# Where the weight halves start in SBUF: a fixed offset modulo 512 bytes for each of two matmul forms

## The chip, the cores and the metric

One Trainium2 chip, one of its cores. The metric is the device time in microseconds (us) of one execution of the whole kernel. The kernel before was timed three times: median 2776.59 us, from 2774.45 to 2779.73.

## The reference, cut to what matters

Two transformer blocks over 256 tokens of width 2048, all in float32. The first has an adaptive-norm modulation, a recurrent branch, a sliding-window attention branch and a gated feed-forward; the second has a gated linear attention and another gated feed-forward. Nearly all the arithmetic is products of the activations with large weight matrices:

```python
h = modulate(rms_norm(x, norm1_g[l]), sh1, sc1)
proj = h @ w_in[l] + b_in[l]                       # 2048 x 11264
...
merged = gate_lru * (y_lru @ w_lru_out[l]) + gate_attn * (y_attn @ w_attn_out[l])
x = x + g1 * (merged @ w_o[l])
h2 = modulate(rms_norm(x, norm2_g[l]), sh2, sc2)
gate, up = jnp.split(h2 @ w_ffn_in[l], 2, axis=-1)  # 2048 x 2 * 5632
x = x + g2 * ((jax.nn.silu(gate) * up) @ w_ffn_out[l])
...                                                 # second block: proj = h @ w_in (GLA), w_out,
...                                                 # and a second feed-forward of the same sizes
```

The modulation vectors are `silu(c) @ ada_w + ada_b`, a single row times a 2048 x 12288 matrix.

## The kernel before, in words

**The product.** Every big weight matrix is cut into chunks of 512 x 512, which lie in SBUF as `[128, 4, 512]` float32 (tile `raw`, 1 MB). A chunk is loaded by SyncE's queue (`load`, L152) and split into two float32r parts: ScalarE copies a half of the chunk into `hi` (L165), VectorE writes the remainder into `lo` (L167). Each `hi` or `lo` tile is half a chunk, `[128, 2, 512]`, 4096 bytes in each partition. The pools hold three of each of `raw`, `hi` and `lo`. The activations are split in the same way once, in tiles of class `Pair`. A product is then three matmuls: hi by hi, hi by lo, lo by hi, accumulated in PSUM by `accumulate`.

**Two forms.** `accumulate` has two forms.
- *Narrow* (256 moving columns, L189, L191, L193): a 128 x 128 block of the weights is the stationary operand and the 256 tokens of the activations stream through. The stationary operands in order are hi, hi, lo; the streams are the activations' hi, lo, hi. A chunk is 48 matmuls.
- *Wide* (512 moving columns, `tokens=True`, L182 to L184): 128 tokens of the activations are stationary and 512 columns of the weights stream through. The streams in order are the weights' hi, lo, hi. A chunk is 24 matmuls. It is used for the two feed-forward input matrices (PSUM names `fgps`, `fups`), for the values of both attentions (`gvps`, and `e` at L182 to L184).

Every matmul record (PE in the profile) has a weight-load record (PEld) ahead of it, which loads the stationary operand while the matmul before is running.

**Order.** A chunk's load, split and matmuls are issued in program order, chunk after chunk; the pools' buffers let loads and splits run ahead of the matmuls. `high_priority(offset=lead[0])` puts loads and splits ahead in the schedule. Small work (attention, recurrence, norms) is interleaved by the generator tasks that `pump` advances. The modulation's matrix is not multiplied on TensorE: `matvec` loads 512 KB pieces of it into tiles `mvw` (L234; on the POOL queue in the first stage, on SP's after that) and VectorE accumulates them into `mva` (L237, L239), 16 pieces for a strip, then a few one-column matmuls sum the partitions (`mvp`, L251). The pool `mvw` has `MVS = 6` buffers.

**Where tiles begin.** The pools are laid out one behind the other in each partition: `const`, `xpool`, `act` (24 slots of 4096 bytes, which hold the activations' `Pair` tiles), `small`, `mvw` (4096 bytes each), `rawp` (8192 each), `hip`, `lop` (4096 each). All of these sizes but that of `small` are multiples of 512. `small` takes 4096 (`ssq`, two) + 1024 (`std`) + 2048 (`inv`, two) + 256 (`st`, two) + 64 (`invp`, two of 32) + 3 x 1024 (`war`, `warh`, `warl`) + 1024 (`ms4`) + 1024 (`alr`) = 12608 bytes, 320 beyond a multiple of 512. So, modulo 512, all `hi` and `lo` tiles begin 320 bytes behind the activations' tiles, which is the same as 192 bytes ahead of them. The blocks within the tiles are whole multiples of 512 bytes apart, so this holds for every operand of the two forms.

Of the kernel before, what the change touches and what calls it, by code (L numbers as in the profile page):

```python
# [12 lines left out]
F32R = mybir.dt.float32r  # L13
# [5 lines left out]
P = 128  # L19
# [3 lines left out]
NG = NK // 4  # L23
EPS = 1e-6
PREP = 2000
SLOTS, MVS, RAWS, HIS, LOS = 24, 6, 3, 3, 3
NEG = -3.0e38
HEADS = 16
KVH = 4
# [20 lines left out]
def block_pair_kernel(ctx: ExitStack, tc: tile.TileContext, a: dict):  # L50
# [8 lines left out]
    hip = ctx.enter_context(tc.tile_pool(name="hip", bufs=HIS))  # L59
    lop = ctx.enter_context(tc.tile_pool(name="lop", bufs=LOS))  # L60
# [8 lines left out]
    def f32(ap):  # L69
        return ap.bitcast(F32)  # L70
# [79 lines left out]
    def load(ap):  # L150
        raw = rawp.tile([P, 4, 512], F32, tag="raw", name="raw")
        nc.sync.dma_start(raw, ap)  # L152
        return raw

    lead = [0]

    def split(ap):

        parts = []
        with tc.high_priority(offset=lead[0]):  # L160
            raw = load(ap)
            for b in range(2):
                rb = raw[:, 2 * b:2 * b + 2, :]
                hi = hip.tile([P, 2, 512], F32R, tag="hi", name="hi")
                nc.scalar.activation(hi, rb, AF.Copy)  # L165
                lo = lop.tile([P, 2, 512], F32R, tag="lo", name="lo")
                nc.vector.tensor_tensor(lo, rb, f32(hi), ALU.subtract)  # L167
                parts.append((hi, lo))
        return parts

    def accumulate(ps, ap, src, first, last, tokens=False):

        parts = split(ap)
        for kk in range(4):
            hi, lo = parts[kk // 2]
            wk = kk % 2
            fst, lst = first and kk == 0, last and kk == 3
            if tokens:
                for t in range(2):
                    tsl = slice(t * P, (t + 1) * P)  # L180
                    xh, xl = src.hi(kk)[:, tsl], src.lo(kk)[:, tsl]
                    nc.tensor.matmul(ps[t], xh, hi[:, wk, :], start=fst, stop=False)  # L182
                    nc.tensor.matmul(ps[t], xh, lo[:, wk, :], start=False, stop=False)  # L183
                    nc.tensor.matmul(ps[t], xl, hi[:, wk, :], start=False, stop=lst)  # L184
                continue
            for f in range(4):
                wsl = slice(f * P, (f + 1) * P)
                o = ps[f // 2][:, f % 2, :]
                nc.tensor.matmul(o, hi[:, wk, wsl], src.hi(kk), start=fst and f % 2 == 0,  # L189
                                 stop=False, skip_group_check=True)  # L190
                nc.tensor.matmul(o, hi[:, wk, wsl], src.lo(kk), start=False, stop=False,  # L191
                                 skip_group_check=True)
                nc.tensor.matmul(o, lo[:, wk, wsl], src.hi(kk), start=False, stop=lst,  # L193
                                 skip_group_check=True)
# [4 lines left out]
    def project(chunks, src, name, tokens=False):  # L199


        ps = banks(name, tokens)
        n = len(chunks)
        for c in range(n):
            accumulate(ps, chunks[c], src[c], c == 0, c == n - 1, tokens)
            if c < n - 1:
                pump()
        return ps
# [247 lines left out]
    for q in range(NG):  # L456
# [3 lines left out]
        for g, ks in plan[q]:  # L460
# [7 lines left out]
            for k in ks:  # L468
                if g in held:
                    accumulate(ps, a["w_in"][g, k], h[k], k == 0, k == NG - 1, tok)  # L470
                else:
                    accumulate(ps, a["w_in"][g, k], h[k], k == ks[0], k == ks[-1])
                for st in ahead[:share]:
                    st()
                if ahead and len(ahead) <= share:
                    next_h()
                ahead = ahead[share:]
                lead[0] = PREP
                if q == NG - 1 and k < ks[-1]:
                    pump()  # L480
# [585 lines left out]
```

## Time and profile before

| What | Value |
|---|---|
| median of three runs | 2776.59 us |
| the profiled execution's own time | 2775.35 us |
| its span, first to last instruction | 2773.6 us |
| granted TensorE clock, mean | 0.999 |
| PE (matmuls) | 2710.8 us, 98% of the span, 18612 records |
| PEld (weight loads) | 2489.2 us, 90% |
| DVE | 1784.8 us, 64% |
| ACT | 1321.3 us, 48% |
| HBM read over the span | 597.06 MB |

How to read it: the span is what the profiler saw between the first and the last instruction, 1.75 us less than that execution's own time. Matmul records overlap, since each is shown from its start to its modelled end behind the array; how fast the matmuls really follow each other is seen from the starts of consecutive records, called the *step* below, and not from their durations.

### The profile page before, as it was taken

How to read it: one execution, taken by the hardware profiler on the slowest of the kernel's cores; microseconds unless marked ns; L12 is line 12 of the kernel's file. 1: busy time of each engine (PE TensorE's matmuls, PEld its weight loads, DVE VectorE, ACT ScalarE, POOL GpSimd, SP SyncE). 2: the span in 40 equal slices, each digit the busy share in tenths (PEclk: the TensorE clock that was granted, in tenths of full speed). 3: DMA queues.
4: the chain of work that ended last, by engine and by line, in shares of the span. 5: the costliest groups of instructions: out<-in, count | busy, mean ns of one | idle time of the engine just before them, and what ended most of it. 6: DMA issues, size and time to landing. Idle time of an engine off the chain costs nothing.

```text
span 2773.6 us, 43912 instructions
## 1 busy us (share of the span) xinstructions
PE 2710.8 (98%) x18612; PEld 2489.2 (90%) x18612; DVE 1784.8 (64%) x2000; ACT 1321.3 (48%) x1531; POOL 25.7 (1%) x52
## 2 busy tenths in 40 slices
PE   4999999999999999999999999999999999999999
PEld 4999899999999788899888999899988889988899
DVE  8887966977876865444444677866654444444544
ACT  3446537873445444434444555555554443344443
POOL 1100000000000000000000000000000000000000
PEclk9999999999999999999999999999999999999999
DMA  9974784768875776555555544445555555555554
GB/s 364 368 301 149 261 324 175 282 241 324 326 283 181 271 259 217 180 190 193 183 192 186 190 169 168 147 144 182 192 188 182 183 190 189 198 182 189 185 196 160
DMA packets 100165, 602.00 MB, mean 217 GB/s; under 512 B 11120, under 2 KB 11632, under 8 KB 40576
## 3 DMA queue, kind: packets, MB, share of 16 engines
q1 hardware_dynamic: 93056, 574.03, 58.2%
q0 software_dynamic: 6912, 25.17, 2.3%
q8 instruction: 145, 2.38, 0.3%
q14 instruction: 52, 0.43, 0.0%
HBM read 597.06 MB, written 2.10 MB: 216 GB/s over the span
## 4 chain that ended last, share of the span: by engine, by line
PE 91%; DVE 5%; ACT 1%; issue 1%; DMA 1%; SPq 0%; DVEq 0%; ACTq 0%
PE fops L189 6%; PE fops L191 6%; PE fops L193 6%; PE fgps L184 6%; PE fgps L183 6%; PE fgps L182 6%; PE fups L184 5%; PE fups L183 5%; PE fups L182 5%; DVE lo L167 2%; PE part L189 2%; PE part L191 2%; PE part L193 2%; DVE mva L239 1%; DMA mvw<-ada_w 1%
## 5 line engine op out<-in xcount | busy, mean ns | idle before, releaser
L167 DVE TENSOR_TENSOR lo<-raw,hi 128x1024 fp32r<-128x1024 f32 x928 | 1134.4, 1223 | 899.3 <-ACT hi L165 897.5
L165 ACT ACTIVATE hi<-raw 128x1024 fp32r<-128x1024 f32 x928 | 982.8, 1060 | 1285.8 <-PE fups L184 280.6
L189 PE MATMUL fops<-hid,hi 128*128 128x256 f32 x1408 | 389.0, 276 | 0.0
L193 PE MATMUL fops<-hid,lo 128*128 128x256 f32 x1408 | 388.8, 276 | 0.0
L191 PE MATMUL fops<-hid,hi 128*128 128x256 f32 x1408 | 388.8, 276 | 0.0
L183 PE MATMUL fups<-lo,h 128*128 128x512 f32 x704 | 275.9, 392 | 0.9 <-DVE lo L167 0.9
L184 PE MATMUL fups<-hi,h 128*128 128x512 f32 x704 | 276.7, 393 | 0.0
L182 PE MATMUL fups<-hi,h 128*128 128x512 f32 x704 | 274.2, 390 | 0.0
L184 PE MATMUL fgps<-hi,h 128*128 128x512 f32 x672 | 264.9, 394 | 0.0
L182 PE MATMUL fgps<-hi,h 128*128 128x512 f32 x672 | 264.6, 394 | 0.0
L191 PEld LDWEIGHTS fops<-hid,hi 128*128 128x128 f32 x1408 | 264.3, 188 | 0.0
L189 PEld LDWEIGHTS fops<-hid,hi 128*128 128x128 f32 x1408 | 264.3, 188 | 0.0
L193 PEld LDWEIGHTS fops<-hid,lo 128*128 128x128 f32 x1408 | 264.3, 188 | 0.0
L183 PE MATMUL fgps<-lo,h 128*128 128x512 f32 x672 | 263.3, 392 | 0.0
L239 DVE SCALAR_TENSOR_TENSOR mva<-mvw,cact,mva 128x1024 f32<-128x1024 f32 x180 | 230.2, 1279 | 18.7 <-DMA mvw<-ada_w 17.0
L183 PEld LDWEIGHTS fups<-lo,h 128*128 128x128 f32 x704 | 132.2, 188 | 31.3 <-DVE lo L167 1.3
L182 PEld LDWEIGHTS fups<-hi,h 128*128 128x128 f32 x704 | 132.2, 188 | 29.3
L184 PEld LDWEIGHTS fups<-hi,h 128*128 128x128 f32 x704 | 132.3, 188 | 27.4
L183 PEld LDWEIGHTS fgps<-lo,h 128*128 128x128 f32 x672 | 126.3, 188 | 27.4
L182 PEld LDWEIGHTS fgps<-hi,h 128*128 128x128 f32 x672 | 126.3, 188 | 26.3
L184 PEld LDWEIGHTS fgps<-hi,h 128*128 128x128 f32 x672 | 126.3, 188 | 26.0
L189 PE MATMUL part<-h,hi 128*128 128x256 f32 x512 | 145.6, 284 | 0.1
(322 smaller groups left out, 5440.6 us busy)
## 6 DMA issues: line engine op xcount, KB each, us to landing
raw<-w_in SPq DMA_DIRECT2D x88, 1024.0 KB, 4.9
raw<-w_ffn_in SPq DMA_DIRECT2D x88, 1024.0 KB, 4.8
raw<-ffn_w_gu SPq DMA_DIRECT2D x88, 1024.0 KB, 4.8
mvw<-ada_w SPq DMA_DIRECT2D x144, 512.0 KB, 6.5
raw<-gla_w_in SPq DMA_DIRECT2D x48, 1024.0 KB, 4.8
raw<-w_ffn_out SPq DMA_DIRECT2D x44, 1024.0 KB, 4.9
raw<-ffn_w_down SPq DMA_DIRECT2D x44, 1024.0 KB, 4.9
mvw<-ada_w POOLq DMA_DIRECT2D x48, 512.0 KB, 8.4
```

What stands on the lines that cost most here:

```text
L165: nc.scalar.activation(hi, rb, AF.Copy)
L167: nc.vector.tensor_tensor(lo, rb, f32(hi), ALU.subtract)
L182: nc.tensor.matmul(ps[t], xh, hi[:, wk, :], start=fst, stop=False)
L183: nc.tensor.matmul(ps[t], xh, lo[:, wk, :], start=False, stop=False)
L184: nc.tensor.matmul(ps[t], xl, hi[:, wk, :], start=False, stop=lst)
L189: nc.tensor.matmul(o, hi[:, wk, wsl], src.hi(kk), start=fst and f % 2 == 0, stop=False, skip_group_check=True)
L191: nc.tensor.matmul(o, hi[:, wk, wsl], src.lo(kk), start=False, stop=False, skip_group_check=True)
L193: nc.tensor.matmul(o, lo[:, wk, wsl], src.hi(kk), start=False, stop=lst, skip_group_check=True)
L239: nc.vector.scalar_tensor_tensor(state["acc"], w, col(k), state["acc"], ALU.mult, ALU.add)
```

## The change

The `hi` and `lo` tiles become 1152 elements long (4608 bytes, nine times 512) and only 1024 of them are used, from an offset that depends on the form. In the narrow form `hi` starts at 0 and `lo` at 32 elements (128 bytes). In the wide form both start at 48 elements (192 bytes). So, modulo 512, the narrow `hi` stays 192 bytes ahead of the activations, the narrow `lo` is 64 bytes ahead of them, and the wide `hi` and `lo` begin level with them. The six longer tiles take 3 KB more in each partition; `MVS` goes from 6 to 5, which frees 4 KB. The count, the operands' shapes and the order of matmuls, loads and splits in the program are the same.

```diff
-SLOTS, MVS, RAWS, HIS, LOS = 24, 6, 3, 3, 3
+SLOTS, MVS, RAWS, HIS, LOS = 24, 5, 3, 3, 3
...
-    def split(ap):
+    def halfbuf(pool, name, tokens):
+        t = pool.tile([P, 1024 + P], F32R, tag=name, name=name)
+        at = 48 if tokens else {"hi": 0, "lo": 32}[name]
+        return t[:, at:at + 1024].rearrange("p (b n) -> p b n", b=2)
+
+    def split(ap, tokens=False):
...
-                hi = hip.tile([P, 2, 512], F32R, tag="hi", name="hi")
+                hi = halfbuf(hip, "hi", tokens)
                 nc.scalar.activation(hi, rb, AF.Copy)
-                lo = lop.tile([P, 2, 512], F32R, tag="lo", name="lo")
+                lo = halfbuf(lop, "lo", tokens)
                 nc.vector.tensor_tensor(lo, rb, f32(hi), ALU.subtract)
...
-        parts = split(ap)
+        parts = split(ap, tokens)
```

## The prediction

> **What bounds the kernel.** I read the page's busy times and clock first, then the groups of instructions, then the timeline of PE alone (for the step from one matmul's start to the next), then the waits.
>
> ```profile
> span 2773.6 us, 43912 instructions
> PE 2710.8 (98%) x18612; PEld 2489.2 (90%) x18612; DVE 1784.8 (64%) x2000; ACT 1321.3 (48%) x1531; POOL 25.7 (1%) x52
> PEclk9999999999999999999999999999999999999999
> L167 DVE TENSOR_TENSOR lo<-raw,hi 128x1024 fp32r<-128x1024 f32 x928 | 1134.4, 1223 | 899.3 <-ACT hi L165 897.5
> L165 ACT ACTIVATE hi<-raw 128x1024 fp32r<-128x1024 f32 x928 | 982.8, 1060 | 1285.8 <-PE fups L184 280.6
> ```
>
> PE is busy in 98% of the span at full clock, and the two splitting engines each stand idle for some 900 us or more: VectorE behind ScalarE, ScalarE behind the matmuls that free its buffers. So the step of the matmuls sets the time. Nothing that the change does to the split's own speed reaches the end before DVE, at 64%, runs out of room.
>
> How many matmuls there are of each form comes from the groups, with shapes kept apart:
>
> ```profile
> L189 PE MATMUL fops<-hid,hi 128*128 128x256 f32 x1408 | 389.0, 276 | 0.0
> L189 PE MATMUL lops<-yr,hi 128*128 128x256 f32 x256 | 72.0, 281 | 0.0
> L189 PE MATMUL glps<-h,hi 128*128 128x256 f32 x256 | 72.0, 281 | 0.0
> L191 PE MATMUL wops<-m,hi 128*128 128x256 f32 x256 | 71.9, 281 | 0.0
> L191 PE MATMUL ups<-h,hi 128*128 128x256 f32 x256 | 71.2, 278 | 0.0
> L191 PE MATMUL part<-h,hi 128*128 128x256 f32 x512 | 143.0, 279 | 0.0
> L183 PE MATMUL fups<-lo,h 128*128 128x512 f32 x704 | 275.9, 392 | 0.9 <-DVE lo L167 0.9
> L183 PE MATMUL fgps<-lo,h 128*128 128x512 f32 x672 | 263.3, 392 | 0.0
> L183 PE MATMUL gvps<-lo,h 128*128 128x512 f32 x128 | 50.1, 392 | 0.0
> L183 PE MATMUL e<-lo,h 128*128 128x512 f32 x32 | 12.6, 394 | 0.0
> L183 PE MATMUL fgps<-lo,gx 128*128 128x512 f32 x32 | 12.6, 392 | 0.0
> ```
>
> L183 is one of three wide lines: (704 + 672 + 128 + 32 + 32) x 3 = 4,704 wide matmuls, 196 chunks. The 928 splits are 464 chunks, so 268 are narrow: x 48 = 12,864. The last column to look at is the mean duration: 276 ns for `fops`, 281 for the same shape in `lops`, `glps`, `wops`, and 278 or 279 for `ups` and `part`. The timeline shows that this goes with the step. Its first and last lines, over four stretches without a break:
>
> ```profile
> 1159.82 0.28 PE L191 MATMUL fops<-hid,hi 128*128 128x256 f32 x1
> ...
> 1165.94 0.28 PE L191 MATMUL fops<-hid,hi 128*128 128x256 f32 x1
> ...
> 799.79 0.28 PE L189 MATMUL wops<-m,hi 128*128 128x256 f32 x1
> ...
> 805.92 0.28 PE L191 MATMUL wops<-m,hi 128*128 128x256 f32 x1
> ...
> 1299.71 0.39 PE L184 MATMUL fgps<-hi,h 128*128 128x512 f32 x1
> ...
> 1308.87 0.39 PE L182 MATMUL fups<-hi,h 128*128 128x512 f32 x1
> ...
> 200.79 0.40 PE L183 MATMUL e<-lo,h 128*128 128x512 f32 x1
> ...
> 204.99 0.40 PE L183 MATMUL e<-lo,h 128*128 128x512 f32 x1
> ```
>
> There are 54, 52, 40 and 18 steps between these lines: 6.12/54 = 113.3 ns, 6.13/52 = 117.9 ns, 9.16/40 = 229.0 ns, 4.20/18 = 233.3 ns. So each form has two steps, a better and a worse one, 4 to 5 ns apart, though in both the operands stand at the same offset modulo 512. Which one runs is not a matter of that offset alone; a stretch falls into one and stays there. The worse narrow one holds all of `lops`, `glps` and `wops` (nine groups of 256, 2,304 matmuls) and, by means of 278 and 279 between 276 and 281, about half of `ups`, `gps` and `part` (another 1,100 to 1,600); I take 3,400.
>
> The form sum: 12,864 x 113.3 = 1457 us, 3,400 x 4.6 = 16, 4,704 x 229.0 = 1077, together 2550 of the 2773.6; the opening and the small work are the rest and the change doesn't touch their operands.
>
> **The change part by part.** What could be had at all is bounded by two other kinds of matmul in the same trace: `lrps`, narrow streams with a load of only 16 columns, and `ss3p`/`ss4p`, full float32, whose 256 columns come at half the rate and so stream as long as 512 wide ones.
>
> ```profile
> 1647.06 0.28 PE L787 MATMUL lrps<-h,warl 128*16 128x256 f32 x1
> ...
> 1648.98 0.28 PE L786 MATMUL lrps<-h,warh 128*16 128x256 f32 x1
> ...
> 1630.49 0.59 PE L294 MATMUL ss3p<-ss,onesd 128*128 128x256 f32 x2
> ...
> 1631.78 0.59 PE L295 MATMUL ss4p<-ss,onesd 128*128 128x256 f32 x2
> ```
>
> `lrps`: 17 steps in 1.92 us, 112.9 ns, within the reading's error the better narrow step. Its stationary blocks are 64 bytes each, one behind the other, so they begin at every multiple of 64 modulo 512 in turn, and the step does not follow. `ss3p`: six records in 1.29 us, 215 ns.
>
> *Narrow, hi left and lo moved by 128 bytes (L193's load).* The better step of 113.3 is what `lrps` has with an eighth of the weight read, so I see nothing to win there: 0. What can go is the worse step: 3,400 x 4.6 ns = 15.6 us, if the new place of `lo` keeps the stream out of it. On the other side, all narrow matmuls could fall into it: (12,864 - 3,400) x 4.6 = +43.5 us. I take -15.6, the end that a third of the way would still bring beyond the timing's noise, because the worse step is a matter of how load and stream stand to each other, and the change sets exactly that.
>
> *Wide, both parts level with the stationary activations (L182 to L184).* The nearest rows are the two steps of this form itself, and twice the better narrow step: 226.6. At that rate the wide matmuls save 229.0 - 226.6 = 2.4 ns, x 4,704 = 11 us. The far end is `ss3p`'s 215: 14 ns, 66 us. On the other side stands the worse wide step: +4.3 ns, 20 us. I take -11, as the row nearest in rate of reading is the narrow stream, not the half-rate one.
>
> *MVS 6 to 5.* Piece k of a strip is now loaded when piece k-5 has been used, one VectorE step of about 1.28 us later. On SP the wait also holds up the `raw` loads queued behind it.
>
> ```profile
> PE mvp L251 <- DVE mva L239: 36.7, 3, 34.4
> DVE mva L239 <- DMA mvw<-ada_w: 17.0, 13, 4.1
> POOL mvw L234 <- DVE mva L239: 95.9, 45, 27.2
> SPq L234 <- DVE mva L239: 47.2, 28, 4.7
> SPq L152 <- DVE lo L167: 2328.9, 453, 17.2
> PE gkps L193 <- DVE lo L167: 2.3, 3, 0.9
> ```
>
> Of PE's 36.7 us behind the modulation 34.4 are the opening, where one strip must be summed before any product; the other two waits are 2.3 us together. The opening can move by up to one VectorE step, 1.3 us. In twelve strips at most 12 x 1.28 = 15 us could show, if PE waited at each; it waits at almost none. A `raw` load stands 2328.9/453 = 5.1 us for its buffer on average, so an SP wait that grows from 4.7 us at most by 1.3 is mostly covered; with that cover gone it would be PE's wait on `lo`, 2.3 us in the largest row now. One load fewer in flight could also leave `raw` a little more of the DMA: -1. I take +1, ends -1 and +15.
>
> *Longer tiles, other addresses in the split.* ScalarE and VectorE write the same 1024 elements, 928 times each; taken at 0, hidden by the idle 899 and 1286 us above. Even 5% more on VectorE's 1134 us would be 57 us of its own idle time.
>
> Sum: -15.6 - 11 + 1 = -25.6. The profiled execution took 2775.35 us (1.75 beyond its span), so it would take 2749.8; the median of the runs is 1.24 above that execution, which makes 2751.
>
> Against the trace stands a rule of the Trainium skill, "TensorE: Matmul & The Clock Gate", Back-to-back issue gap: N/2.4 + 2.5 ns for a single warm matmul, 109.2 and 215.8 ns here. The trace shows 113.3 and 229.0 instead, and 215 only in the half-rate form. By that rule, were both forms to reach it, the estimate would be -53 - 16 - 62 + 1 = -130 us, about 2646; `lrps` speaks against its narrow part.
>
> **The rivals.**
> - *Nothing happens.* The start modulo 512 doesn't matter to PE at all, and the time is that of before with one `mvw` buffer less: 2776.6 + 1 = 2778. For it: `lrps` goes through all eight starts at one step, and the two steps of each form occur at one and the same offset. Against it: those loads are short, and something that depends on how load and stream stand to each other makes the worse step. The Trainium skill has a rule that gives this outcome, "SBUF — State Buffer", Who interferes with whom: PE's stream and its weight load have a read port each, and PE waits on nobody. The two steps at equal shape, count and clock are hard to square with it.
> - *Slower: the wide form locks into its worse step.* With stream and load level, both begin on the same part of a 512-byte period within a few ns of each other. If that is the bad stand, each wide matmul costs 233.3 as in `e` at 200 us: 4,704 x 4.3 = +20 us, +1 for MVS: 2798. Against it: the better step is by far the commoner in this form. It decides alone from 5.5/4,704 = 1.2 ns a matmul on. If the narrow form falls into its worse step as well, 2841.
> - *Much faster: the wide stream loses its whole surplus* and steps at 215 like the half-rate one: -66 - 15.6 + 1, 2696. Against it: full-rate streams never step better than at 112.9 for half the columns, twice which is 226.
>
> **How the numbers follow.** Chances: the forecast with gains of some 6 to 40 us 0.37; much faster 0.12; nothing 0.25; slower by the wide form 0.17; slower in both 0.09. A change below 0.2%, 5.5 us, can't be told from none (the three runs lie 5.3 us apart). From "nothing", 0.02 may end on either side by chance of which stretches fall into the worse step, and 0.01 of the slower ones ends within: faster 0.50, same 0.24, slower 0.26. Predicted: 2751, with 2735 to 2771 as its own range. The range of all reaches from 2715 (which leaves out the most of "much faster") to 2798 (which leaves out "slower in both").
>
> **What would show it.** Right: `lops`, `glps` and `wops` at a mean of 276 ns; narrow steps of 113.3 throughout; wide steps of about 226 to 227; PE's waits as they are. Wrong: wide durations up towards 397 and steps of 233 (the slower rival); both forms' steps unmoved (nothing happens); a wide step below 220 or a narrow one below 112 (more to gain than I allow). A new PE wait on `mvp` in the opening or on `lo` while strips are loaded would mean that I priced the lost buffer too low.

## The result, and the profile after

The changed kernel takes 2761.12 us in the median (2757.35 to 2761.36), against 2777.45 us for the kernel before measured beside it (2774.45 to 2779.73): a ratio of 0.9939, with a 95% interval from 0.9921 to 0.9956. It is faster by 16 us, 0.6%; the prediction said 2751, 10 us less. The profiled execution took 2761.13 us, with a span of 2759.4 us, 14.2 less than before.

The page's busy times and its largest VectorE group. All lines of the product stand 8 lower in the changed file: narrow L197, L199, L201; wide L190 to L192; the split L173 and L175; the modulation's sum L247.

```profile
span 2759.4 us, 43921 instructions
PE 2691.7 (98%) x18612; PEld 2478.1 (90%) x18612; DVE 1783.9 (65%) x2000; ACT 1321.7 (48%) x1531; POOL 25.7 (1%) x52
L175 DVE TENSOR_TENSOR lo<-raw,hi 128x1024 fp32r<-128x1024 f32 x928 | 1134.4, 1223 | 871.2 <-ACT hi L173 869.2
```

PE is still busy in 98% of a shorter span. The split costs VectorE the same 1223 ns a tile, so the new addresses cost it nothing. Its idle time ahead of this group fell from 899 to 871 us, and its waits for pieces of the modulation matrix grew by 13 us (below).

The groups by shape of the kernel after (busy time and mean ns of one, after the bar):

```profile
L197 PE MATMUL fops<-hid,hi 128*128 128x256 f32 x1408 | 389.0, 276 | 0.0
L197 PE MATMUL lops<-yr,hi 128*128 128x256 f32 x256 | 70.8, 276 | 0.0
L197 PE MATMUL glps<-h,hi 128*128 128x256 f32 x256 | 70.9, 277 | 0.0
L199 PE MATMUL wops<-m,hi 128*128 128x256 f32 x256 | 70.7, 276 | 0.0
L199 PE MATMUL ups<-h,hi 128*128 128x256 f32 x256 | 70.7, 276 | 0.0
L191 PE MATMUL fups<-lo,h 128*128 128x512 f32 x704 | 273.9, 389 | 0.0
L191 PE MATMUL fgps<-lo,h 128*128 128x512 f32 x672 | 262.2, 390 | 0.0
```

`lops`, `glps` and `wops` came down from 281 ns to 276 or 277, where `fops` already was. The wide groups went from 392 to 389 or 390. The timeline of PE gives the step behind that: first and last line of three stretches of the kernel after without a break, in `glps`, `wops` and the wide form, with 55, 55 and 40 steps between them.

```profile
699.74 0.28 PE L197 MATMUL glps<-h,hi 128*128 128x256 f32 x1
...
705.97 0.28 PE L199 MATMUL glps<-h,hi 128*128 128x256 f32 x1
...
799.74 0.28 PE L199 MATMUL wops<-m,hi 128*128 128x256 f32 x1
...
805.97 0.28 PE L201 MATMUL wops<-m,lo 128*128 128x256 f32 x1
...
1299.77 0.39 PE L192 MATMUL fups<-hi,h 128*128 128x512 f32 x1
...
1308.84 0.39 PE L190 MATMUL fups<-hi,h 128*128 128x512 f32 x1
```

6.23/55 = 113.3 ns twice, where `wops` had 117.9 before; 9.07/40 = 226.8 ns, where it was 229.0.

Taken over all records of the two traces, from each matmul's start to the next one's (a narrow step between 116 and 130 ns counted as the worse one):

| | before | after | difference |
|---|---|---|---|
| narrow: steps in all | 1484.1 us | 1473.4 us | -10.7 us |
| narrow: how many in the worse step | 3,390 of 12,807 | 319 of 12,809 | |
| narrow: pauses of over 130 ns, in all | 30.0 us | 32.2 us | +2.2 us |
| narrow: mean of the better step | 113.34 ns | 113.34 ns | |
| wide: steps in all | 1068.9 us | 1059.0 us | -9.9 us |
| wide: mean step | 229.0 ns | 226.9 ns | |
| everything else on PE | 182.1 us | 187.9 us | +5.9 us |
| first matmul | | | 0.6 us later |

The rows of both forms' steps in all, of everything else and of the first matmul add up to -14.1, the change of the span. The first holds two things: the worse steps, 3,390 at 4.5 ns above the better one before and 319 at 5.6 after, which is 15.1 less 1.8, so -13.3; and the longer pauses. About 23 us were gained and 9 given back. Some of what gives them back is seen in PE's and VectorE's waits, totals in us, times and the longest:

```profile
PE mvp L259 <- DVE mva L247: 38.0, 3, 35.0
PE aops L201 <- DVE lo L175: 2.5, 2, 1.9
DVE mva L247 <- DMA mvw<-ada_w: 30.4, 26, 3.1
```

The opening wait on `mvp` has grown from 36.7 us to 38.0, VectorE stands 30.4 us instead of 17.0 for pieces of the modulation matrix, and a wait of `aops` on `lo` has grown from 0.4 to 2.5 us. The longest of its two comes about so (start and duration in us; in brackets, what the engine stood idle for before):

```profile
354.92 1.06 ACT L173 ACTIVATE hi<-raw 128x1024 fp32r<-128x1024 f32 x1 [1.65 <-PE aops L199]
360.11 1.28 DVE L247 SCALAR_TENSOR_TENSOR mva<-mvw,cact,mva 128x1024 f32<-128x1024 f32 x1 [3.13 <-DMA mvw<-ada_w]
361.31 1.22 DVE L175 TENSOR_TENSOR lo<-raw,hi 128x1024 fp32r<-128x1024 f32 x1
362.59 0.39 PE L201 MATMUL aops<-ya,lo 128*128 128x256 f32 x1 [1.92 <-DVE lo L175]
```

The chunk was there in time: counted in order, this copy `hi` is the one that this `lo` needs, and it was done at 355.98 us. But VectorE stood 3.13 us for a piece of the modulation matrix, whose sum comes ahead of the split in its order, and PE stood 1.92 us behind that.

The other large part is the granted clock. The trace of the kernel before has one stretch of 3.4 us at half the clock (from 132 us), the trace of the kernel after has four (from 82, 134, 321 and 960 us). Three more of them are 3 x 3.4 x 0.5 = 5 us, an estimate. Two of them are shown with the next experiment.

### The profile page after: what moved, and what is told of

Read it like the earlier page. It is cut to its first block, busy times and chain, and to the rows that moved or that the text cites. A ratio compares the mean times of both kernels' runs of the same rounds, so it can differ in the third digit from the quotient of the medians.

```text
span 2759.4 us, 43921 instructions
## 1 busy us (share of the span) xinstructions
PE 2691.7 (98%) x18612; PEld 2478.1 (90%) x18612; DVE 1783.9 (65%) x2000; ACT 1321.7 (48%) x1531; POOL 25.7 (1%) x52
## 4 chain that ended last, share of the span: by engine, by line
PE 88%; DVE 5%; DMA 3%; issue 3%; ACT 1%; POOL 0%; SPq 0%; DVEq 0%; POOLq 0%; ACTq 0%
PE fgps L191 6%; PE fgps L190 6%; PE fgps L192 6%; PE fops L197 6%; PE fops L201 6%; PE fops L199 6%; PE fups L192 5%; PE fups L190 5%; PE fups L191 5%; DMA mvw<-ada_w 3%; DVE lo L175 2%; PE part L199 1%; PE part L197 1%; PE part L201 1%; ACT hi L173 1%
## 5 line engine op out<-in xcount | busy, mean ns | idle before, releaser
L175 DVE TENSOR_TENSOR lo<-raw,hi 128x1024 fp32r<-128x1024 f32 x928 | 1134.4, 1223 | 871.2 <-ACT hi L173 869.2
L173 ACT ACTIVATE hi<-raw 128x1024 fp32r<-128x1024 f32 x928 | 983.1, 1060 | 1263.2 <-PE fups L192 274.5
L197 PE MATMUL fops<-hid,hi 128*128 128x256 f32 x1408 | 389.0, 276 | 0.0
L201 PE MATMUL fops<-hid,lo 128*128 128x256 f32 x1408 | 388.9, 276 | 0.0
L199 PE MATMUL fops<-hid,hi 128*128 128x256 f32 x1408 | 388.8, 276 | 0.0
L190 PE MATMUL fups<-hi,h 128*128 128x512 f32 x704 | 274.0, 389 | 0.0
L192 PE MATMUL fups<-hi,h 128*128 128x512 f32 x704 | 273.9, 389 | 0.0
L190 PE MATMUL fgps<-hi,h 128*128 128x512 f32 x672 | 264.7, 394 | 0.0
L199 PEld LDWEIGHTS fops<-hid,hi 128*128 128x128 f32 x1408 | 264.3, 188 | 0.0
L201 PEld LDWEIGHTS fops<-hid,lo 128*128 128x128 f32 x1408 | 264.3, 188 | 0.0
L197 PEld LDWEIGHTS fops<-hid,hi 128*128 128x128 f32 x1408 | 264.3, 188 | 0.0
L192 PE MATMUL fgps<-hi,h 128*128 128x512 f32 x672 | 263.1, 391 | 0.0
L247 DVE SCALAR_TENSOR_TENSOR mva<-mvw,cact,mva 128x1024 f32<-128x1024 f32 x180 | 230.5, 1280 | 32.3 <-DMA mvw<-ada_w 30.4
L190 PEld LDWEIGHTS fups<-hi,h 128*128 128x128 f32 x704 | 132.1, 188 | 27.5
L192 PEld LDWEIGHTS fups<-hi,h 128*128 128x128 f32 x704 | 132.1, 188 | 27.5
L192 PEld LDWEIGHTS fgps<-hi,h 128*128 128x128 f32 x672 | 126.3, 188 | 26.0
L190 PEld LDWEIGHTS fgps<-hi,h 128*128 128x128 f32 x672 | 126.5, 188 | 25.0
L197 PE MATMUL part<-h,hi 128*128 128x256 f32 x512 | 145.4, 284 | 0.0
```

The lines of the kernel that those rows point to most:

```text
L247: nc.vector.scalar_tensor_tensor(state["acc"], w, col(k), state["acc"], ALU.mult, ALU.add)
```

## The experiments

Two theories stood at the start. One: the two places act separately, each on its own form, and the lost `mvw` buffer takes a part of the gain back. The rivals: the gain is the longer tiles or a reshuffle of the schedule, so that any change of the kind shifts stretches between the two steps; or one of the places brings it all. (The longer tiles by themselves are answered below: `narrow_only` and `wide_only` both have them, and each leaves the step of the other form as it was.) "Before" is measured beside each kernel on the same chip; for the first four its median was 2779.75 us.

### The change with its buffer back

```diff
-SLOTS, MVS, RAWS, HIS, LOS = 24, 5, 3, 3, 3
+SLOTS, MVS, RAWS, HIS, LOS = 24, 6, 3, 3, 3
```

> The new offsets in both forms, with the sixth mvw buffer back. Theory (offsets give the whole gain, the lost buffer takes some of it back, by the trace about 4 to 5 us of waits): ratio to the kernel before 0.9925, some 2757 us; narrow steps of 113.3 and wide of 226.9 as with the change; PE's waits of some 2 us on lo in aops and the longer opening gone. Rival (the buffer costs only the 1 us that was predicted, the extra waits are chance): 0.994, the same as the change. Rival (the gain came from the schedule with five buffers): no gain left, 1.000.

Measured: 2755.35 us, ratio 0.9911 [0.9898, 0.9924]; span 2753.5 us; 316 narrow matmuls in the worse step, wide step 226.91 ns. The steps are those of the kernel after, so the 5.9 us between the two spans lie outside them, in the waits and in the clock. The waits of this kernel, to be read against those above:

```profile
PE mvp L259 <- DVE mva L247: 36.3, 3, 33.9
DVE mva L247 <- DMA mvw<-ada_w: 19.6, 14, 4.1
PE lops L201 <- DVE lo L175: 1.4, 1, 1.4
PE aops L201 <- DVE lo L175: 0.5, 1, 0.5
```

Five stretches in both traces, the kernel after first, this one second. Columns: window, its length, busy time (and matmuls) of PE, of PEld, DVE, ACT, POOL, then granted clock, DMA share and GB/s.

```profile
0.00:100.00 100.00, 59.13 (x436) 56.86 (x437) 81.63 (x118) 39.82 (x52) 12.56 (x28) 0.98 0.92 351
345.00:400.00 55.00, 52.51 (x459) 52.07 (x458) 40.83 (x37) 20.24 (x20) 0.00 (x0) 1.00 0.86 320
950.00:1000.00 50.00, 48.11 (x210) 39.61 (x209) 28.40 (x26) 19.77 (x21) 0.00 (x0) 0.97 0.72 258
82.50:85.50 3.00, 3.00 (x15) 3.00 (x15) 2.42 (x7) 0.51 (x1) 0.00 (x0) 0.50 1.06 423
960.00:962.50 2.50, 2.50 (x11) 2.10 (x11) 1.37 (x3) 0.80 (x2) 0.00 (x0) 0.50 0.81 301
```

```profile
0.00:100.00 100.00, 60.81 (x449) 58.38 (x450) 83.76 (x120) 40.73 (x53) 14.06 (x30) 1.00 0.94 364
345.00:400.00 55.00, 54.53 (x480) 54.27 (x479) 42.43 (x40) 20.87 (x20) 0.00 (x0) 1.00 0.88 332
950.00:1000.00 50.00, 49.21 (x221) 40.22 (x219) 26.07 (x25) 20.43 (x22) 0.00 (x0) 1.00 0.69 244
82.50:85.50 3.00, 3.00 (x29) 3.00 (x28) 2.96 (x8) 0.84 (x2) 0.00 (x0) 1.00 1.04 416
960.00:962.50 2.50, 2.50 (x13) 2.07 (x12) 1.23 (x1) 0.84 (x2) 0.00 (x0) 1.00 0.66 264
```

With five buffers PE gets through 13, 21 and 11 matmuls fewer in the first three stretches. At 345 to 400 us that is the wait of `aops` on a late `lo`. In the opening and at 950 to 1000 us it is in good part the clock: the last two rows lie inside stretches of 3.4 us at half the clock in the kernel after, and at full clock here. This trace has two such stretches (from 132 and 320 us), two fewer, which is 2 x 3.4 x 0.5 = 3.4 of the 5.9 us by the same estimate. Whether the buffer brings them is not shown. The traces with five buffers have three (`mvs5_only`), four and five of them, those with six none to four (four in `narrow_only`). Nor is the longer opening wait on `mvp` shown to be the buffer's: the repeat of this kernel below has it at 37.5 us with six.

### The buffer alone

The kernel before with `MVS = 5` and nothing else.

> The kernel before with five mvw buffers and nothing else. Theory: 4 us slower (ratio 1.0015), narrow groups glps, lops, wops still at a mean of 281 ns, wide steps still 229. Rival (which stretches fall into the worse step is chance that any new schedule reshuffles): the narrow groups change their means, some 281 become 276 or the other way, and the time moves by up to 14 us either way with no offset touched.

Measured: 2782.15 us, ratio 1.0009 [0.9999, 1.0018]: at most 5 us, and not told apart from nothing.

```profile
L191 PE MATMUL lops<-yr,hi 128*128 128x256 f32 x256 | 71.9, 281 | 0.0
PE mvp L251 <- DVE mva L239: 39.4, 3, 34.6
DVE mva L239 <- DMA mvw<-ada_w: 27.1, 20, 3.6
```

`lops` keeps its 281 ns, so the loss of a buffer doesn't free the narrow form. The same two waits grow as in the kernel after. Yet 4,745 narrow matmuls are in the worse step instead of 3,390, above all since `ups` and `gps`, partly in the better one before, now run in the worse throughout. So far the rival is borne out: a new schedule does shift stretches, here for the worse.

### One place at a time

```diff
-        at = 48 if tokens else {"hi": 0, "lo": 32}[name]
+        at = 0 if tokens else {"hi": 0, "lo": 32}[name]      # narrow_only, MVS = 6
...
+        at = 48 if tokens else 0                             # wide_only, MVS = 6
```

> Narrow lo moved by 128 bytes, wide hi and lo left where they were, six buffers. Theory: the worse narrow step goes (3,390 matmuls x 4.5 ns): 14 to 15 us less, ratio 0.9948, wide steps still 229.0. Rival (the wide form's new start also clears the narrow one, through the state in which it leaves PE): 281 ns stays in some of glps, lops, wops, ratio above 0.997.

Measured: 2766.01 us, ratio 0.995 [0.9938, 0.9962]; 340 narrow matmuls in the worse step, wide step 228.95 ns. As expected. `wops` (54 steps) and the wide form (40 steps) of this kernel:

```profile
799.82 0.28 PE L199 MATMUL wops<-m,hi 128*128 128x256 f32 x1
...
805.94 0.28 PE L199 MATMUL wops<-m,hi 128*128 128x256 f32 x1
...
1299.83 0.39 PE L190 MATMUL fups<-hi,h 128*128 128x512 f32 x1
...
1308.98 0.39 PE L191 MATMUL fups<-lo,h 128*128 128x512 f32 x1
```

113.3 and 228.8 ns: the narrow form is mended, the wide one is as it was.

> Wide hi and lo level with the activations, narrow hi and lo both left where they were, six buffers. Theory: wide steps 226.9 instead of 229.0, 4,704 x 2.1 ns = 10 us less, ratio 0.9964; glps, lops and wops still at 281 ns. Rival (chance): wide steps unmoved or narrow groups changed.

Measured: 2779.09 us, ratio 0.9997 [0.9987, 1.0007]: no gain, where one of 10 us was expected. Yet the wide step of this kernel did fall; here the wide form (40 steps) and `wops` (53 steps):

```profile
1299.77 0.39 PE L191 MATMUL fgps<-lo,h 128*128 128x512 f32 x1
...
1308.84 0.39 PE L192 MATMUL fups<-hi,h 128*128 128x512 f32 x1
...
799.72 0.28 PE L201 MATMUL wops<-m,lo 128*128 128x256 f32 x1
...
805.96 0.28 PE L199 MATMUL wops<-m,hi 128*128 128x256 f32 x1
```

226.8 ns, worth 10 us, and 117.7 in `wops`. Over the whole trace 5,683 narrow matmuls are in the worse step against 3,390 in before's: (5,683 - 3,390) x 4.5 = 10 us back. With `lo` at its old place the share of the worse step differs from one kernel's profiled execution to the next (3,390, 4,745 with the buffer alone, 5,683 here), while with `lo` moved it stayed at 297 to 340 in all six that have it so. That this share swallowed the gain is shown for the profiled execution; for the others there is only the median. So the two effects don't add as they would if each form had one step: the wide gain is seen in the total only once the narrow form is kept out of its worse step. The share is not mere chance either. In all four kernels with the old place (`apart_256`, below, is the fourth) `lops` and `wops` run in the worse step throughout, and `fops` in the better but for its last 958 matmuls in `wide_only`.

### What about the place counts

The next four kernels also move the wide starts from projection to projection, so that one trace holds many of them; `MVS` is 6, and only the first number of the narrow form and the wide rule differ. All compute the full result. Each was timed in a single execution, against 2780.73 us for the kernel before on that chip; what counts in them are the steps.

```diff
+    turn = [0]
+    def wide_at(name):
+        n = turn[0] % 8
+        return 16 * n                                         # both_moved
+        return 48 if name == "hi" else (48 + 16 * n) % 128    # swapped
+        return 32 + 4 * n                                     # apart_256
+        return 48 if name == "lo" else (48 + 16 * n) % 128    # apart_64
...
-        at = 48 if tokens else {"hi": 0, "lo": 32}[name]
+        at = wide_at(name) if tokens else {"hi": 32, "lo": 32}[name]   # both_moved
+        at = wide_at(name) if tokens else {"hi": 32, "lo": 0}[name]    # swapped
+        at = wide_at(name) if tokens else {"hi": 0, "lo": 64}[name]    # apart_256
+        at = wide_at(name) if tokens else {"hi": 0, "lo": 16}[name]    # apart_64
...
+        turn[0] += tokens
```

> Narrow: hi and lo both start 32 elements in, so both 64 bytes ahead of the activations and level with each other. Theory A (what counts is the distance between hi and lo, the two weight blocks loaded one behind the other): the worse narrow step stays, 3,000 to 6,000 matmuls at 117.8 ns. Theory B (what counts is where lo's load begins against the streaming activations): it goes, about 320 matmuls as in the kernels with lo moved alone. Wide: hi and lo level with each other, from 0 to 448 bytes by steps of 64, another start for each projection in turn; start 192 is level with the activations. Theory: 226.9 ns at 192 and its worse neighbours 229 or more; if only 0 (the kernel before) is bad, seven starts give 226.9; rival (half-rate bound): one start gives 220 or less.

2807.59 us; 11,011 narrow matmuls in the worse step, at 117.8 ns. With `hi` and `lo` moved together it is far worse than before: moving `lo` is not enough by itself.

> Narrow: hi 32 elements in and lo at 0, 128 bytes apart the other way round. Theory A (distance): the worse narrow step is gone, about 320 matmuls. Theory B (lo against the activations, now back at its old place): it stays, 3,000 to 6,000. Wide: hi level with the activations, lo moved from 0 to 448 bytes behind it by steps of 64, another for each projection. Theory: 226.9 at distance 0; at other distances the steps behind a lo differ from those behind a hi, by up to 6 ns.

2812.18 us; 8,963 in the worse step, at 118.9 ns. The distance is again 128 bytes, but with the two places exchanged the worse step stays. A distance alone, counted without its sign, would be blind to the exchange, so that theory falls; and modulo 256, which is shown below to be the period, 128 either way is the same distance.

> Narrow: lo 256 bytes behind hi, 64 bytes past the activations' start. Theory A: distance 256 is not 0, worse step gone (about 320 matmuls). Theory B: gone too, if only the old place is bad. If it stays, 128 is a special distance. Wide: hi and lo level with each other in steps of 16 bytes from 128 to 240 bytes, level with the activations at 192. Theory: 226.9 at 192; if the start within a 64-byte line counts, the steps off a multiple of 64 are longer.

2794.83 us; 4,604 in the worse step, as in the kernels with the old place. A `lo` that is moved by 256 bytes behaves like one that isn't moved.

> Narrow: lo 64 bytes behind hi. Theories A and B alike: worse step gone or cut (0 to 1,000 matmuls), if 64 bytes are enough. Wide: lo level with the activations, hi moved from 0 to 448 bytes behind by steps of 64. Theory: 226.9 at 0; hi streams twice in three, so its distance costs twice what lo's does.

2822.58 us; 11,455 in the worse step, at 118.7 ns. Both theories had it gone; both were wrong. The groups of `fops` in the four, in the order above (one fence each), and of `lops` in the third:

```profile
L205 PE MATMUL fops<-hid,hi 128*128 128x256 f32 x1408 | 392.2, 279 | 0.0
```

```profile
L205 PE MATMUL fops<-hid,hi 128*128 128x256 f32 x1408 | 396.4, 282 | 0.0
```

```profile
L203 PE MATMUL fops<-hid,hi 128*128 128x256 f32 x1408 | 389.0, 276 | 0.0
L205 PE MATMUL lops<-yr,hi 128*128 128x256 f32 x256 | 71.9, 281 | 0.0
```

```profile
L203 PE MATMUL fops<-hid,hi 128*128 128x256 f32 x1408 | 398.1, 283 | 0.0
```

The third has before's pattern, 276 in `fops` and 281 in `lops`; in the others `fops` has left its 276 as well.

For the wide form the same traces give its step by place. Two stretches of `apart_256`: 44 steps 32 bytes ahead of level and 45 steps level.

```profile
1409.62 0.40 PE L197 MATMUL fups<-lo,h 128*128 128x512 f32 x1
...
1419.89 0.40 PE L196 MATMUL fups<-hi,h 128*128 128x512 f32 x1
...
1457.71 0.39 PE L197 MATMUL fups<-lo,h 128*128 128x512 f32 x1
...
1467.91 0.39 PE L197 MATMUL fups<-lo,h 128*128 128x512 f32 x1
```

10.27/44 = 233.4 and 10.20/45 = 226.7 ns in one kernel, some 40 us apart, with nothing else of the matmuls changed but where the streams begin. The eight places of `both_moved`, as the mean step over the matmuls of all projections at a place (steps under 245 ns), `hi` and `lo` at the same place; "bytes" is the start of the weights' parts less that of the activations, modulo 512:

| bytes | 0 | 64 | 128 | 192 | 256 | 320 (before) | 384 | 448 |
|---|---|---|---|---|---|---|---|---|
| step, ns | 227.2 | 229.1 | 232.5 | 233.3 | 227.2 | 229.1 | 232.7 | 233.3 |

The second half repeats the first: the period is 256 bytes, not 512. Closer to level the step is no smaller (`apart_256`): 16 bytes behind 231.7, 32 behind 233.3, 16 ahead 234.9. No place was below 226.9. With only one of the two parts moved (`swapped`, `apart_64`) it is 227.1 to 227.3 where both are level modulo 256, and 229.0 to 234.3 elsewhere. The wide form too can have two steps at one place: 16 bytes ahead three projections ran at 233.3 and three at 236.4 to 236.6, and at the old place `e` stepped at 231.2 in the kernel before and at 228.9 in `narrow_only`.

### Period and level, in full timings

Before's median beside the last four kernels was 2780.21 us. Two rivals were left for the narrow form: that a place level with the activations is best in both forms, or that what is best for a stream of weights is not for a load of them.

> The changed kernel once more, timed on the same chip beside the one with six mvw buffers. Theory (the lost buffer costs 4 to 8 us): 5.8 us slower than that one, as between the two traces so far; ratio to the kernel before 0.993. Rival (the buffer costs 1 us): the two within 2 us.

2764.35 us, ratio 0.9938 [0.9924, 0.9951]; 297 in the worse step. The result above is repeated.

> New offsets with six mvw buffers, once more: ratio to the kernel before 0.991; 5.8 us ahead of the changed kernel by the theory, under 2 by the rival.

2756.15 us, ratio 0.9912 [0.9899, 0.9926]. Between these two the sixth buffer goes with 2764.35 - 2756.15 = 8.2 us; their intervals just touch, one of the five runs with five buffers took 2755.80, and the pair of spans above says 5.9. In the old placement it was 2.4 us (`mvs5_only`), not told apart from nothing.

```diff
-        at = 48 if tokens else {"hi": 0, "lo": 32}[name]
+        at = 112 if tokens else {"hi": 64, "lo": 96}[name]    # moved_256, MVS = 6
...
+        at = 48                                               # level_both, MVS = 6
```

> As the version with six buffers, every hi and lo moved on by 256 bytes in both forms. Theory (what counts is the start modulo 256): nothing changes, wide 226.9 ns, about 320 matmuls in the worse narrow step, ratio 0.991. Rival (modulo 512 counts in the narrow form): thousands of matmuls in the worse narrow step, 8 to 50 us more.

2755.77 us, ratio 0.9912 [0.9899, 0.9926]; 322 in the worse step, wide 226.90 ns. All starts 256 bytes on, and nothing changes: the period holds in both forms.

> Narrow hi and lo level with the activations too, as in the wide form, six buffers. Theory 1 (level is the good place in both forms): narrow steps 113.3 throughout, ratio 0.991. Theory 2 (the narrow form needs hi and lo apart, since with hi and lo level the worse step came up in every run so far): 3,000 to 11,000 matmuls at 117.8, 13 to 50 us more, ratio 0.996 to 1.009.

2826.81 us, ratio 1.0164 [1.015, 1.0178]; 12,703 narrow matmuls in the worse step, at 120.0 ns, the wide step unchanged at 226.91. A group of `fops`, and 51 of its steps, in this kernel:

```profile
L197 PE MATMUL fops<-hid,hi 128*128 128x256 f32 x1408 | 398.8, 283 | 0.0
```

```profile
1199.77 0.28 PE L201 MATMUL fops<-hid,lo 128*128 128x256 f32 x1
...
1205.89 0.28 PE L201 MATMUL fops<-hid,lo 128*128 128x256 f32 x1
```

6.12/51 = 120.0 ns in the product that runs at the better step throughout in the kernel before.

What is best for the wide stream is the worst that was seen for the narrow load: 47 us over the kernel before, 71 over the best placement. The narrow places tried, modulo 256:

| `hi` less activations | `lo` less activations | kernels | narrow matmuls in the worse step |
|---|---|---|---|
| 64 | 64 | before, buffer alone, `wide_only`, `apart_256` | 3,390; 4,745; 5,683; 4,604 |
| 64 | 192 | after, `narrow_only`, `moved_256` and repeats | 297 to 340 |
| 192 | 192 | `both_moved` | 11,011 |
| 192 | 64 | `swapped` | 8,963 |
| 64 | 128 | `apart_64` | 11,455 |
| 0 | 0 | `level_both` | 12,703 |

These are six of the sixteen pairs at multiples of 64 bytes. Which mechanism makes a place good is not shown by any run; only that both places count, that they count modulo 256, and that the two forms want different ones.

## Why the prediction was nearly right

- *What bounds the kernel*: right. The splits kept their time, and what the matmuls' steps lost came off the span, less what the waits and the clock gave back.
- *Narrow, -15.6*: right in what happens, and nearly in size. 3,400 worse steps were taken, there were 3,390; 319 remained, so -13.3. The better step gained nothing, as taken (113.34 ns in both). That the sign came out was in part luck: the working priced both ends, -15.6 and +43.5, and no row of the trace told which this place would bring. Of the six pairs in the table above it is the only one without thousands of worse steps. And what `lrps` shows, one step at all eight starts, holds only for its 16-column loads: `level_both` puts full loads at 120.0 ns by their start alone.
- *Wide, -11*: right in size, 226.9 ns against the 226.6 taken, -9.9 us. That level is the good place was a choice too: two other places of the table, 128 and 192 bytes away, are worse than before's. The bound from `ss3p` at 215 was not approached at any place.
- *MVS, +1 with ends -1 and +15*: the step that was mis-sized, in its way as well as its price. The kernel with five buffers is 5.9 us longer between the profiled spans and 8.2 between the timed medians, so by the spans 4.9 us of the 11.4 by which the change fell short of -25.6 stand here. The prediction looked for the wait on SP's queue, where the 5.1 us that a `raw` load stands for its buffer on average would cover it. The `aops` wait of 1.9 us came another way: the chunk was there, but VectorE stood for a late piece of the modulation matrix with the split behind it. The prediction did name a wait on `lo` as the sign of a price set too low.
- *The clock*: the term that the prediction did not have. It took full clock throughout. Three more stretches at half the clock than in the kernel before are some 5 us of the 11.4, and two of them are 3.4 of the buffer's 5.9, so the two shares overlap. What starts such a stretch isn't shown, nor that the buffer does.
- *What is left*: with six buffers the trace gives -20.1 instead of -26.6: narrow -11.5 (1.8 us of worse steps left and 2.0 of longer pauses), wide -10.8, and 2.4 us more in everything else, of which one more stretch at half the clock than before can be 1.7; the rest was not followed further.
- *"Nothing happens"*: refuted by `narrow_only` and the wide tables. A rule of the Trainium skill that stood behind it, "SBUF — State Buffer", Who interferes with whom, has PE wait on nobody, with a read port each for stream and load. The runs disagree in so far as the same matmuls step at 226.7 or 233.4 ns by their start within one trace; whether a port is the place where they meet, no run shows.
- *"The wide form locks into its worse step"*: refuted for the wide form, where level is the best place (226.9). In the other form level is bad indeed: level narrow loads nearly all run at 120.0.
- *"Much faster"*: refuted at every place tried, of which none stepped below 113.3 and 226.9 ns on average. The rule of the Trainium skill's "TensorE: Matmul & The Clock Gate", Back-to-back issue gap, for a single warm matmul gives 109.2 and 215.8 ns for these columns as an estimate, and no place reached it.
- Both chances and range were built on additive terms. `wide_only` shows that they needn't be: a term of -10 us came to nothing in the total, because the other form's share of the worse step isn't fixed by the wide placement.

The best version is the change with its sixth buffer kept: 0.9911 and 0.9912, some 24 us below before and 6 to 8 below the kernel after.

## What to carry to other kernels

Measure a matmul's cost as the step between starts in the timeline, by group: if equal shapes show two steps, try the placement of the stationary operand against the moving one (0.991 to 1.016 of the time here); one trace with the start swept from product to product compares many places, as it did for the wide form. Don't carry a good place from one form to the other, or from streams to loads: level was best for a stream of weights and the worst of six pairs for a load of them. When a placement costs memory, look at what the lost buffer makes an engine wait for, and at what stands behind that wait in the engine's order: with one of six prefetch buffers fewer the kernel was 6 to 8 us longer, though the queue's average wait looked well covered. And before a difference of a few us between two traces is put down to a change, count the stretches at a lower clock in both.

## What the hardware showed that was not expected

- The step of a float32r matmul depends on the starts of both operands modulo 256 bytes: 226.9 to 234.9 ns for 512 columns, 113.3 to 120.0 ns for 256, as means.
- At one and the same placement the narrow form has two steps, 113.3 and 117.8 ns, and keeps one over long stretches. In four kernels with that placement 3,390 to 5,683 of some 12,807 matmuls were in the worse one. What sets it at the start of a stretch stays open.
- Even the best placements left 113.3 and 226.9 ns, while full float32 at half the rate stepped at 215 ns for as long a stream. Where the surplus goes stays open too.
- The granted clock falls to half for 3.4 us at a time: never in the trace of `level_both`, once in that of the kernel before, four times in that of the kernel after and five times in its repeat. There the narrow step is 213.3 ns (kernel after, 83 to 85 us), 100 ns more than 113.3, but less than twice that.
